# Delta stage of a two-block kernel: inverses by pivot columns, another order of emission, and low weight halves on VectorE instead of GpSimd

## The chip, the cores and the metric

The kernel runs as one program on one core of a Trainium2 chip. The metric is the device time of one execution in microseconds; less is better. The engines are TensorE (PE in the rows; PEld is its weight load), VectorE (DVE), ScalarE (ACT), GpSimd (POOL) and SyncE (SP), which here issues the DMAs. Each engine works through its own instructions in the order that was fixed when the kernel was built, and waits for other engines and DMAs by semaphores.

## The reference

Two blocks act on 512 tokens of 1024 channels, all in float32. The first has Fourier mixing with attention and a gated linear recurrence. The second has a mixer, cross attention to a memory, and a hierarchical mixture of experts. The mixer's first branch, the gated delta rule with 8 heads, is where the change lies. Cut to that:

```python
qkv = silu(causal_depthwise_conv(hn @ w_in[qkv], conv_w))
q, k = l2norm(q), l2norm(k)                 # per head, 128 wide
decay = exp(cum_i - cum_j)                  # lower triangle of a chunk of 64 tokens
a_low = where(strict, (k * beta) @ k.T * decay, 0)
sol = triangular_solve(eye + a_low, [v * beta, k * beta * exp(cum)], lower=True)
for chunk:                                  # sequential over chunks, S is 128 x 128
    v_new = u - w @ S
    o = q_dec @ S + qk_intra @ v_new
    S = S * chunk_decay + k_dec.T @ v_new
y_a = rmsnorm(o) * silu(out_gate)
```

## The kernel before

`stage_c()` (from L1019) is the mixer. Channels lie on the partitions and tokens on the free axis. A projection (`proj`, L280) is eight blocks of 128 input channels, each of three matmuls of 128 x 512, since a float32 weight and input are split into a high and a low half (`mm3`, L268): 24 matmuls into one of three PSUM banks `pj`. Other matmuls go to five banks `pm`.

**Weights.** `wget` (L255) takes the next weight block of the list `cq`, which must hold the blocks in the order in which the code asks for them; it is loaded two blocks ahead (`LC`). `wsplit` (L225) loads 128 x 1024 floats through the SyncE queue into `wr` (4 buffers), ScalarE writes the high half `wh` (L215, 4 buffers), and the difference, the low half `wl` (L217, 3 buffers), is made by VectorE, or by GpSimd for every n-th block when `wpool[0]` is n. The table `WP` sets `wpool` by sub-stage.

**The delta stage** works on two groups of four heads. `ftile(h, t)` projects head h's k (t = 1), q (0) or v (2), and runs the convolution on ScalarE and VectorE: one start `cy` on ScalarE, three multiply-adds `cy` on VectorE, a tanh, and one operation that writes `KQ` or `VF`. `p2a` makes the decay triangle `E` (GpSimd at L1132 and L1144), `p2` transposes `KQ` on TensorE (L1156), and makes the product `MI` of k with [k, q]; its 32 x 32 diagonal blocks go to DRAM (`abd`). `group_thin` works out a row of small factors for the group, `nr` among them, in some twenty operations of 16 or 32 elements a partition.

`inverse(g)` inverts the 128 unit lower triangular blocks of 32 x 32 that a group has, one in each partition: `nr` is transposed on TensorE (L1200), goes through DRAM and comes back as `rb`, the blocks come back as `AB`, and `AB` is scaled by `rb` on VectorE. Then the rows of the inverse `xr` (name `xrow`) are filled, two at a time. It is a Python generator: `over(steps, g)` emits a step of other work (a projection and what follows it), and then as many pieces of the inverse as the table `IV` (`pace`) gives for that kind of step. At the end `xt` goes to DRAM (`xd`) and comes back by eight DMAs as blocks in `X1T`.

`merges(g)` joins the 32-blocks into the inverses of 128-blocks with small matmuls. `chain(g)` is the sequential part, four chunks `c` of 128 tokens: transposes of `VF` (L1302), `vb` on VectorE, the product with `X1T` (L1314), `vn` on ScalarE, the state `St` and the output; each step needs the one before. `ofac`, `og(h)` (the output gate's projection and its `sg`) and `finish(h)` (the `y`) complete a head. `fproj(h)`, `vproj(hp)` and the projections Q are those of the next branch (HGRN); its heads follow in `hhead`. In `vproj` the weight is the moving operand: 96 matmuls of 256 columns.

**What sets the order.** The code's order of emission is not the order on an engine: a scheduler places instructions by their dependencies and an estimate of times as it builds the program, each engine's list apart. `pin()` (L265) keeps what is emitted under it behind the last projection matmul emitted. Work without dependencies on the inverse can so fill TensorE while VectorE inverts, and fill the gaps of the chain ("filler matmuls").

Of the kernel before, what the change touches and what calls it, by code (L numbers as in the profile page):

```python
# [6 lines left out]
F32 = mybir.dt.float32  # L7
# [5 lines left out]
AX = mybir.AxisListType  # L13
# [8 lines left out]
LC = [2]  # L22
IV = [2, 2, 3, 2, 1, 1]
XB = [2, 1]
# [24 lines left out]
TL = [0]  # L49
WP = [3, 1, 0, 1, 0, 0]  # L50
VP = [2]
# [113 lines left out]
def build(tc, a, stages="A", dbg=None):  # L165
# [42 lines left out]
    def mul(o, x, y):  # L208
        dve.tensor_tensor(o, x, y, op=MUL)  # L209
# [55 lines left out]
    def pin(on=True):  # L265
        return tc.issue_after(lastmm[0].ins) if on else ExitStack()
# [752 lines left out]
    def stage_c():  # L1019
# [10 lines left out]
        cq.extend([F_(4, 1), F_(4, 0), F_(4, 2), F_(5, 1), F_(5, 0), F_(5, 2), O_(0), O_(1)])  # L1030
        cq.extend([O_(2), O_(3), F_(6, 1), F_(6, 0), F_(7, 1), F_(7, 0)])
        cq.extend([P_(h) for h in range(4)] + [O_(4), O_(5), O_(6), F_(6, 2), F_(7, 2), O_(7)])
        cq.extend(V_(0) + V_(1) + [Q_(0), Q_(1)] + [Q_(2), Q_(3)] + [P_(h) for h in range(4, 8)] + V_(2))
        for i in range(4):
# [5 lines left out]
        def fproj(h):  # L1040
# [3 lines left out]
            act.activation(TH[h], ps, AF.Tanh, scale=0.5)  # L1044

        with tc.tile_pool(name="cg", bufs=1, reuse_waits="tile") as G:
            RS = ExitStack()
            R2 = RS.enter_context(tc.tile_pool(name="cr", bufs=1, reuse_waits="tile", side="right"))
            AB = R2.tile([128, 32, 32], F32, name="AB")
            vb0, ab = CAB  # L1050
# [146 lines left out]
            def inverse(g):  # L1197
# [226 lines left out]
            steps = [(fproj, 0), (fproj, 1), (fproj, 2), (fproj, 3), (og, 4), (og, 5), (og, 6), (ftile, 6, 2)]  # L1424
            for _ in range(PI[2]):
                st = steps.pop(0)
                st[0](*st[1:])
            p2(7)
# [3 lines left out]
            for _ in range(PI[3]):
                st = steps.pop(0)
                st[0](*st[1:])
            with pin(PI[3]):
# [15 lines left out]
        with tc.tile_pool(name="ch", bufs=1, reuse_waits="tile") as Hh:  # L1451
# [14 lines left out]
            v3 = lambda z: z.rearrange("p (c i) -> p c i", c=4)  # L1466
            VT, LF = {}, {}

            def vproj(hp):
                VT[hp] = R3.tile([128, 4, 256], F32, name="vt", tag="vt", bufs=2)  # L1470
                w = [wget("wci", 4 * k + hp, k) for k in range(2)]
                for tp in range(2):
                    ps = (psm if VP[0] >> hp & 1 else psj)()
                    for t in range(2):
                        tt = 2 * tp + t
                        mm3(ps[:, t * 256:t * 256 + 256],
                            [((X[k][0][:, tt * 128:tt * 128 + 128], X[k][1][:, tt * 128:tt * 128 + 128]),
                              (w[k // 4][0][:, (k % 4) * 256:(k % 4) * 256 + 256],
                               w[k // 4][1][:, (k % 4) * 256:(k % 4) * 256 + 256])) for k in range(8)])
                    act.activation(VT[hp][:, 2 * tp:2 * tp + 2, :], ps.rearrange("p (t n) -> p t n", t=2), AF.Copy)  # L1480

# [797 lines left out]
```

## Time and profile before

| | |
|---|---|
| runs | 2199.89, 2196.14, 2195.3 us; median 2196.14 |
| profiled execution | 2199.17 us; span 2197.3 us |
| TensorE busy in the span | 2104.1 us, 96% |
| VectorE busy | 1306.4 us, 59% |
| ScalarE busy | 866.3 us, 39% |
| GpSimd busy | 250.3 us, 11% |

The span is what the profiler saw from the first to the last instruction; the execution's own time is a little longer. Times in the trace count from the span's start. The change touches the stretch from about 790 to 1160 us: the first group's tiles, the first inverse (from 881), merges(0) and chain(0) (to 999), the second group's last tiles (to 1033), the second inverse (to 1092), merges(1), chain(1) (from 1113) and the start of the next branch (from 1138). In a timeline row "[3.30 <-DVE ort]" is the time the engine stood idle before it, and whose result ended that.

### The profile page before, as it was taken

The page shows a single profiled execution, that of the slowest core. Times are in us where ns is not written, and L with a number is a line of the kernel's source. Part 1 is how long each engine was busy: PE and PEld are TensorE (multiplying, and loading weights), DVE is VectorE, ACT ScalarE, POOL GpSimd, SP SyncE. Part 2 cuts the span into 40 slices and gives each one's busy share as a digit, 9 for nine tenths or more (in the row PEclk, how much of TensorE's full clock was granted, in tenths as well). Part 3 has the DMA queues.
Part 4 walks back from the last instruction along what each step waited for, and adds up shares of the span by engine and source line. Part 5 has one row for each costly group of instructions (what it writes and reads, how often), then busy time and mean ns, then how long its engine had stood idle before and what let it go on. Part 6 is the DMA issues. An engine that isn't in the chain of part 4 may idle for free. (4 is left out here: it accounts for less than half of the span.)

```text
span 2197.3 us, 28137 instructions
## 1 busy us (share of the span) xinstructions
PE 2104.1 (96%) x10806; PEld 1581.4 (72%) x10806; DVE 1306.4 (59%) x2282; ACT 866.3 (39%) x1562; POOL 250.3 (11%) x164
## 2 busy tenths in 40 slices
PE   8899999999999999898899999999999999999997
PEld 6788888788787888686788886888876544444443
DVE  7777677878858866857856454325654333333334
ACT  4444435488848664323236533223442011111002
POOL 3300000300101253423300000100001000000000
PEclk9999999999999999999999999999999999999998
DMA  5422222432322542221311225333426899999993
GB/s 178 129 63 87 68 68 72 144 101 87 115 91 64 174 129 94 70 69 47 105 54 62 80 95 167 108 100 114 133 109 265 346 411 420 420 421 421 421 420 116
DMA packets 96242, 364.65 MB, mean 166 GB/s; under 512 B 19298, under 2 KB 24804, under 8 KB 71652
## 3 DMA queue, kind: packets, MB, share of 16 engines
q1 hardware_dynamic: 94068, 359.36, 44.7%
q10 hardware_dynamic: 2032, 3.41, 0.5%
q8 instruction: 87, 1.43, 0.3%
q14 instruction: 55, 0.45, 0.1%
HBM read 348.56 MB, written 11.55 MB: 164 GB/s over the span
## 5 line engine op out<-in xcount | busy, mean ns | idle before, releaser
L271 PE MATMUL pj<-xh,wh 128*128 128x512 f32 x1136 | 448.6, 395 | 9.4 <-ACT wh L215 3.9
L273 PE MATMUL pj<-xh,wl 128*128 128x512 f32 x1136 | 447.3, 394 | 4.5 <-DVE wl L217 4.5
L272 PE MATMUL pj<-xl,wh 128*128 128x512 f32 x1136 | 445.7, 392 | 0.0
L215 ACT ACTIVATE wh<-wr 128x1024 fp32r<-128x1024 f32 (+1 forms) x269 | 263.1, 981 | 460.0 <-PE pj L272 279.8
L217 DVE TENSOR_TENSOR wl<-wr,wh 128x1024 fp32r<-128x1024 f32 (+1 forms) x242 | 277.8, 1149 | 159.6 <-PE pj L273 69.0
L271 PEld LDWEIGHTS pj<-xh,wh 128*128 128x128 f32 x1136 | 214.7, 189 | 56.3 <-ACT wh L215 5.6
L273 PEld LDWEIGHTS pj<-xh,wl 128*128 128x128 f32 x1136 | 214.6, 189 | 50.3 <-DVE wl L217 6.5
L272 PEld LDWEIGHTS pj<-xl,wh 128*128 128x128 f32 x1136 | 214.5, 189 | 43.5 <-DVE xl L217 0.7
L2046 PE MATMUL pj<-we,xe 128*64 128x512 f32 x1024 | 225.0, 594 | 0.0
L2046 PEld LDWEIGHTS pj<-we,xe 128*64 128x64 f32 x1024 | 71.4, 137 | 140.5 <-issue 137.8
L1991 DVE TENSOR_TENSOR mo<-mo,pm 128x512 f32<-128x512 f32 x128 | 80.9, 683 | 78.6 <-PE pm L1990 78.6
L2046 PE MATMUL pj<-we,hT 128*64 128x512 f32 x512 | 113.4, 595 | 0.4 <-ACT hT L1977 0.4
L2046 PEld LDWEIGHTS pj<-we,hT 128*64 128x64 f32 x512 | 35.4, 137 | 66.8 <-issue 63.9
L217 POOL TENSOR_TENSOR wl<-wr,wh 128x1024 fp32r<-128x1024 f32 x27 | 69.0, 2559 | 117.9 <-PE pj L273 86.6
L1977 ACT ACTIVATE hT<-pm 128x512 f32<-128x512 f32 x16 | 9.6, 598 | 175.7 <-PE pm L1975 175.7
L1939 PE MATMUL pm<-dk,xh 128*128 128x256 f32 x256 | 65.3, 295 | 0.0
L1939 PE MATMUL pm<-dk,xl 128*128 128x256 f32 x256 | 63.8, 289 | 0.0
L1967 ACT ACTIVATE th<-pj,ws 128x512 f32<-128x512 f32 x16 | 11.0, 689 | 126.6 <-PE pj L2046 125.5
L2039 POOL TENSOR_TENSOR we<-mo,we 128x512 f32<-128x512 f32 x4 | 5.0, 1292 | 488.0 <-DVE mo L1991 488.0
L1982 ACT ACTIVATE ye<-pj,ws 128x512 fp32r<-128x512 f32 x32 | 22.0, 689 | 95.3 <-PE pj L2046 95.3
L209 DVE TENSOR_TENSOR th<-th,pj 128x512 f32<-128x512 f32 x16 | 11.0, 688 | 80.1 <-PE pj L2046 80.1
L212 DVE SCALAR_TENSOR_TENSOR cy<-pj,vec,cy 128x509 f32<-128x509 f32 (+2 forms) x72 | 53.6, 744 | 8.5 <-ACT cy L1113 7.5
(622 smaller groups left out, 4335.7 us busy)
## 6 DMA issues: line engine op xcount, KB each, us to landing
we<-in_eg SPq DMA_DIRECT2D x64, 1024.0 KB, 10.3
we<-in_eu SPq DMA_DIRECT2D x64, 1024.0 KB, 10.1
we<-in_ed SPq DMA_DIRECT2D x63, 1024.0 KB, 12.9
wr<-in_wc SPq DMA_DIRECT2D x72, 512.0 KB, 3.6
wr<-in_wa SPq DMA_DIRECT2D x34, 512.0 KB, 3.7
wr<-in_wb SPq DMA_DIRECT2D x32, 512.0 KB, 3.7
wr<-in_wbr SPq DMA_DIRECT2D x16, 512.0 KB, 3.6
wr<-in_wao SPq DMA_DIRECT2D x8, 512.0 KB, 4.2
```

Of the source, the lines that this page charges most:

```text
L209: dve.tensor_tensor(o, x, y, op=MUL)
L212: dve.scalar_tensor_tensor(o, x, s, y, op0=op0, op1=op1)
L215: act.activation(hi, x, AF.Copy, scale=1.0 if scale is None else scale)
L217: (eng or dve).tensor_tensor(lo, x, f(hi), op=SUB)
L271: pe.matmul(ps, lh, rh, start=first and i == 0, stop=False)
L272: pe.matmul(ps, lh, rl, start=False, stop=False)
L273: lastmm[0] = pe.matmul(ps, ll, rh, start=False, stop=last and i == n - 1)
L1939: pe.matmul(ps[:, (c & 1) * 256:(c & 1) * 256 + n], HN[t, c // 4][i % 2][:, (c % 4) * 128:(c % 4) * 128 + 128], dk[t // 2][:, t % 2, :n], ...
L1967: act.activation(th, pg, AF.Tanh, scale=ws[:, 2:3])
L1982: act.activation(Y[0], py, AF.Copy, scale=ws[:, 1:2])
L1991: dve.tensor_tensor(acc[t, hf], acc[t, hf], ps, op=ADD)
L2046: last[0] = pe.matmul(ps[64 * e:64 * e + 64], lhs(k, e), wt[k // 2][:, 2 * e + k % 2, :], start=k == 0, stop=k == n - 1)
```

## The change

Three things change in the delta stage. No matmul is added or taken away.

1. `inverse` fills `xr` column by column: for each pivot j, all rows below j take the product of column j of `AB` with row j of `xr`, added in one product (L209) and one addition. That is 62 operations on (31 - j)(j//2 + 1) elements in place of sixteen products and sixteen sums on 4m x m elements (m from 1 to 16) and of the first pairing of `AB` (one product, one addition, two fills). The product's tile moves from the tag `St` to the tag `tmp`, of which there are seven buffers.
2. `WP` turns GpSimd's share of the low halves off after the first group's tiles: 17 low halves go to VectorE.
3. The order of emission: `fproj(0)` and `fproj(1)` stand inside chain(0), `fproj(2)`, `fproj(3)`, `finish(0)` and `finish(1)` among the last tiles of the second group; `ftile(7, 2)` and `vproj(0)` go into the second inverse, ahead of merges(1); `p2(6)`, `p2(7)` and the first piece of each inverse are pinned. `vproj`'s result shares two buffers with `AB`.

```diff
-IV = [2, 2, 3, 2, 1, 1]
+IV = [2, 2, 3, 2, 1, 2]
-WP = [3, 1, 0, 1, 0, 0]
+WP = [3, 0, 0, 0, 0, 0]
...
+        def vproj(hp):
+            VT[hp] = R2.tile([128, 4, 256], F32, name="vt", tag="vt", bufs=2)
...
-            AB = R2.tile([128, 32, 32], F32, name="AB")
+            AB = R2.tile([128, 32, 32], F32, name="AB", tag="vt", bufs=2)
...
                 mul(AB, AB, rb.unsqueeze(1).to_broadcast([128, 32, 32]))
-                ABf = AB.rearrange("p j i -> p (j i)")
-                dve.memset(ABf[:, 0:1024:33], 0.0)
-                pt = G.tile([128, 32, 16], F32, name="prod", tag="tmp", bufs=NT[0])
-                mul(pt, AB[:, :, 0::2], ABf[:, 1:1024:66].unsqueeze(1).to_broadcast([128, 32, 16]))
-                dve.tensor_tensor(AB[:, :, 1::2], AB[:, :, 1::2], pt, op=ADD)
-                dve.memset(ABf[:, 0:1024:33], 1.0)
...
-                prod = G.tile([128, 1024], F32, name="prod", tag="St", bufs=1)
-                for i in range(0, 32, 2):
-                    n, m = i + 2, i // 2 + 1
-                    pr = prod[:, :m * 2 * n].rearrange("p (c r j) -> p c r j", c=m, r=2)
-                    mul(pr, xr[:, :n, :m].rearrange("p j c -> p c j").unsqueeze(2).to_broadcast([128, m, 2, n]),
-                        AB[:, :n, i:i + 2].rearrange("p j r -> p r j").unsqueeze(1).to_broadcast([128, m, 2, n]))
-                    dve.reduce_sum(xr[:, i:i + 2, :m].rearrange("p r c -> p c r"), pr, axis=AX.X)
-                    yield
+                prod = G.tile([128, 512], F32, name="prod", tag="tmp", bufs=NT[0])
+                for j in range(31):
+                    n, m = 31 - j, j // 2 + 1
+                    pr = prod[:, :n * m].rearrange("p (i c) -> p i c", c=m)
+                    mul(pr, AB[:, j, j + 1:32].unsqueeze(2).to_broadcast([128, n, m]),
+                        xr[:, j:j + 1, :m].to_broadcast([128, n, m]))
+                    dve.tensor_tensor(xr[:, j + 1:, :m], xr[:, j + 1:, :m], pr, op=ADD)
+                    if j & 1:
+                        yield
+                yield
...
+            ftile(4, 0)
             inv = inverse(0)
-            if PI[0]:
-                ftile(4, 0)
-            with pin(PI[0]):
+            with pin():
                 adv(inv, 1)
...
-            over(((ftile, 4, 0),) * (1 - PI[0]) + ((ftile, 4, 2), (ftile, 5, 1), (p2, 4), (p2a, 5), (ftile, 5, 0), (ftile, 5, 2)) +
-                 (((og, 0), (p2, 5)) if PI[1] else ((p2, 5), (og, 0))) + ((og, 1), (og, 2), (og, 3)), inv)
+            over(((ftile, 4, 2), (ftile, 5, 1), (p2, 4), (p2a, 5), (ftile, 5, 0), (ftile, 5, 2), (og, 0), (og, 1),
+                  (p2, 5), (og, 2), (og, 3)), inv)
             adv(inv, 99)
             wpool[0] = WP[2]
             merges(0)
-            adv(chain(0), 99)
-            fc = ofac(0)
+            ch = chain(0)
+            adv(ch, 1)
+            fproj(0)
+            adv(ch, 1)
+            fproj(1)
+            adv(ch, 99)
             ftile(6, 1)
             p2a(6)
             ftile(6, 0)
+            fc = ofac(0)
             ftile(7, 1)
-            p2(6)
+            with pin():
+                p2(6)
             p2a(7)
             ftile(7, 0)
...
+            finish(0, fc)
+            fproj(2)
+            with pin():
+                p2(7)
             group_thin(1)
+            finish(1, fc)
+            fproj(3)
             wpool[0] = WP[3]
             inv = inverse(1)
...
-            over([(finish, h, fc) for h in range(4)] + steps, inv)
+            over(((finish, 2, fc), (finish, 3, fc), (og, 4), (og, 5), (og, 6), (ftile, 6, 2), (ftile, 7, 2), (vproj, 0)), inv)
             adv(inv, 99)
             wpool[0] = WP[4]
-            ftile(7, 2)
...
             merges(1)
             adv(chain(1), 99)
             og(7)
```

How instructions move shows best in three places. In the order's rows a number stands first, then the line, the operation, and what it writes and reads.

GpSimd, from the first group's last tiles to merges(1), before (`m1t` belongs to merges, the four `Gm` and `E` to p2a):

```order
69 L217 TENSOR_TENSOR wl<-wr,wh 128x1024 x3
70 L1132 TENSOR_TENSOR Gm<-c_78,gls_7361 128x512
71 L1132 TENSOR_TENSOR Gm<-c_78,gls_7362 128x512
72 L217 TENSOR_TENSOR wl<-wr,wh 128x1024
73 L1144 TENSOR_TENSOR E<-E,c_78 128x512
74 L217 TENSOR_TENSOR wl<-wr,wh 128x1024 x4
75 L1244 TENSOR_TENSOR m1t<-MI,c_78 128x512 x4
76 L1218 MEMSET X1T 128x2048
77 L1132 TENSOR_TENSOR Gm<-c_78,gls_7361 128x512
78 L1132 TENSOR_TENSOR Gm<-c_78,gls_7362 128x512
79 L1144 TENSOR_TENSOR E<-E,c_78 128x512
80 L217 TENSOR_TENSOR wl<-wr,wh 128x1024
```

and the same stretch after the change:

```order
65 L1147 TENSOR_TENSOR Gm<-c_78,gls_7361 128x512
66 L1147 TENSOR_TENSOR Gm<-c_78,gls_7362 128x512
67 L1159 TENSOR_TENSOR E<-E,c_78 128x512
68 L1147 TENSOR_TENSOR Gm<-c_78,gls_7361 128x512
69 L1147 TENSOR_TENSOR Gm<-c_78,gls_7362 128x512
70 L1159 TENSOR_TENSOR E<-E,c_78 128x512
71 L1255 TENSOR_TENSOR m1t<-MI,c_78 128x512 x4
72 L1227 MEMSET X1T 128x2048
73 L1147 TENSOR_TENSOR Gm<-c_78,gls_7361 128x512
74 L1147 TENSOR_TENSOR Gm<-c_78,gls_7362 128x512
75 L1159 TENSOR_TENSOR E<-E,c_78 128x512 x2
76 L1255 TENSOR_TENSOR m1t<-MI,c_78 128x512 x4
```

All the `wl` of this stretch are gone from GpSimd's list (seven more follow in row 82 of before); the others keep their order.

VectorE at the start of the first inverse (`AB` by `rb` is its first operation, `prod` and `xrow` are the recurrence), before:

```order
1046 L209 TENSOR_TENSOR AB<-AB,rb 128x1024
1047 L1212 MEMSET AB 128x32
1048 L209 TENSOR_TENSOR prod<-AB 128x512
1049 L212 SCALAR_TENSOR_TENSOR cy<-pj,vec,cy 128x509
1050 L1215 TENSOR_TENSOR AB<-AB,prod 128x512
1051 L212 SCALAR_TENSOR_TENSOR cy<-pj,vec,cy 128x510
1052 L1216 MEMSET AB 128x32
1053 L212 SCALAR_TENSOR_TENSOR cy<-pj,vec,cy 128x511
1054 L209 TENSOR_TENSOR prod<-xrow,AB 128x4
1055 L1227 TENSOR_REDUCE xrow<-prod 128x2
1056 L209 TENSOR_TENSOR prod<-xrow,AB 128x16
1057 L1227 TENSOR_REDUCE xrow<-prod 128x2x2
```

and after:

```order
1055 L209 TENSOR_TENSOR AB<-AB,rb 128x1024
1056 L212 SCALAR_TENSOR_TENSOR cy<-pj,vec,cy 128x511
1057 L209 TENSOR_TENSOR prod<-AB,xrow 128x31
1058 L1236 TENSOR_TENSOR xrow<-xrow,prod 128x31
1059 L209 TENSOR_TENSOR prod<-AB,xrow 128x30
1060 L217 TENSOR_TENSOR wl<-wr,wh 128x1024
1061 L212 SCALAR_TENSOR_TENSOR VF<-cy 128x512
1062 L1236 TENSOR_TENSOR xrow<-xrow,prod 128x30
1063 L212 SCALAR_TENSOR_TENSOR cy<-pj,vec,cy 128x509
1064 L209 TENSOR_TENSOR prod<-AB,xrow 128x58
1065 L212 SCALAR_TENSOR_TENSOR cy<-pj,vec,cy 128x510
1066 L1236 TENSOR_TENSOR xrow<-xrow,prod 128x29x2
```

The recurrence now begins right behind the scaling, in pairs of a product and an addition, and low halves (`wl`) stand between them; there are six of them up to `xt` in the first inverse, and four in the second.

TensorE in chain(1), its second chunk (`vb,X1T` and `St,KQ` are the chain's, L271 to L273 filler matmuls of a projection), before:

```order
4602 L271 MATMUL pj<-wh,xh 128x256
4603 L272 MATMUL pj<-wl,xh 128x256
4604 L273 MATMUL pj<-wh,xl 128x256
4605 L271 MATMUL pj<-wh,xh 128x256
4606 L272 MATMUL pj<-wl,xh 128x256
4607 L1314 MATMUL pm<-vb,X1T 128x128
4608 L1320 MATMUL pm<-St,KQ 128x128
4609 L1314 MATMUL pm<-vb,X1T 128x128 x3
4610 L1320 MATMUL pm<-St,KQ 128x128 x3
4611 L273 MATMUL pj<-wh,xl 128x256
4612 L1325 MATMUL pm<-vn,KD 128x128 x4
4613 L1336 MATMUL pm<-vn,MI 128x128 x4
```

and after (chain lines have moved by eleven):

```order
4665 L1336 MATMUL pm<-vn,KD 128x128 x4
4666 L1347 MATMUL pm<-vn,MI 128x128 x4
4667 L1313 MATMUL pm<-c_78,VF 128x128 x4
4668 L1319 MATMUL pm<-St,KQ 128x128 x4
4669 L1325 MATMUL pm<-vb,X1T 128x128
4670 L1331 MATMUL pm<-St,KQ 128x128
4671 L1325 MATMUL pm<-vb,X1T 128x128 x2
4672 L1331 MATMUL pm<-St,KQ 128x128
4673 L1325 MATMUL pm<-vb,X1T 128x128
4674 L1331 MATMUL pm<-St,KQ 128x128 x2
4675 L1336 MATMUL pm<-vn,KD 128x128 x4
4676 L1347 MATMUL pm<-vn,MI 128x128 x4
```

The fillers are gone from here, and from the three other chunks too: before, 47 filler matmuls stand in chain(1), after, none. In chain(0) it is the other way: seven before, all in its first chunk, and 30 after, in all four.

## Rows read from the trace of the kernel before

**Rows 1.** page, part 1: busy us (share of the span), instructions

```profile
PE 2104.1 (96%) x10806; PEld 1581.4 (72%) x10806; DVE 1306.4 (59%) x2282; ACT 866.3 (39%) x1562; POOL 250.3 (11%) x164
```

**Rows 2.** stretches: us; busy (count) of PE, PEld, DVE, ACT, POOL; clock

```profile
881.00:954.00 73.00, 65.09 (x280) 52.98 (x279) 61.27 (x82) 23.64 (x58) 33.32 (x15) 0.95 0.26 77
975.40:999.60 24.20, 21.21 (x163) 18.79 (x161) 14.24 (x40) 9.63 (x38) 2.04 (x2) 1.00 0.07 23
999.60:1033.30 33.70, 24.85 (x111) 19.97 (x112) 28.37 (x60) 14.91 (x54) 12.33 (x7) 0.95 0.15 44
1033.30:1092.10 58.80, 52.37 (x250) 44.58 (x249) 48.91 (x57) 14.78 (x20) 20.39 (x9) 0.94 0.35 108
1112.90:1137.70 24.80, 24.80 (x202) 23.66 (x201) 14.65 (x38) 10.87 (x39) 0.55 (x2) 1.00 0.14 43
```

**Rows 3.** PE's waits, 880 to 1150 us: total us, times, longest

```profile
PE pm L1156 <- DVE KQ L212: 7.5, 4, 3.0
PE pj L271 <- DVE cy L212: 6.4, 1, 6.4
PE pm L1200 <- DVE ort L209: 3.3, 1, 3.3
PE pj L271 <- DVE oss L1357: 2.7, 1, 2.7
PE pm L1200 <- DVE nr L212: 2.3, 1, 2.3
```

**Rows 4.** shorter stretches, columns as in rows 2

```profile
885.00:888.50 3.50, 3.50 (x10) 2.73 (x9) 0.11 (x1) 0.00 (x0) 0.00 (x0) 0.51 0.47 107
1011.40:1014.80 3.40, 2.91 (x9) 2.58 (x10) 2.27 (x5) 1.15 (x8) 0.00 (x0) 0.50 0.47 159
1083.00:1089.90 6.90, 5.18 (x24) 5.21 (x25) 5.49 (x7) 2.58 (x4) 2.66 (x2) 0.51 0.55 143
1050.00:1060.00 10.00, 10.00 (x46) 8.26 (x45) 9.50 (x15) 3.73 (x5) 5.21 (x2) 1.00 0.40 131
```

**Rows 5.** timeline of POOL and DVE: start us, us, engine, line, operation

```profile
880.86 2.38 POOL L217 TENSOR_TENSOR wl<-wr,wh 128x1024 fp32r<-128x1024 f32 x1 [1.45 <-DVE rstg L212]
881.06 2.22 DVE L209 TENSOR_TENSOR rstg<-rsyg 128x32 f32<-128x32 f32 x1
1008.30 0.69 DVE L209 TENSOR_TENSOR VF<-VF,ort 128x512 f32<-128x512 f32 x1
1008.91 2.84 DVE L212 SCALAR_TENSOR_TENSOR KQ<-cy 128x512 f32<-128x512 f32 x1
```

**Rows 6.** POOL's groups, 880 to 1150 us: busy us, mean ns; idle, releaser

```profile
L217 POOL TENSOR_TENSOR wl<-wr,wh 128x1024 fp32r<-128x1024 f32 x16 | 42.0, 2625 | 61.8 <-PE pj L273 47.3 <-issue 7.5 <-DVE ort L209 3.8
L1144 POOL TENSOR_TENSOR E<-E,c 128x512 f32<-128x512 f32 x3 | 4.8, 1584 | 8.1 <-ACT E L1143 8.1
```

**Rows 7.** DVE's groups, 1040 to 1079 us (second inverse)

```profile
L209 DVE TENSOR_TENSOR prod<-xrow,AB 128x4 f32<-128x4 f32 (+15 forms) x16 | 19.7, 1233 | 0.5
L1227 DVE TENSOR_REDUCE xrow<-prod 128x2 f32<-128x4 f32 (+15 forms) x16 | 8.7, 544 | 0.5
L209 DVE TENSOR_TENSOR AB<-AB,rb 128x1024 f32<-128x1024 f32 x1 | 3.5, 3467 | 6.9 <-DMA AB<-abd 6.9
```

**Rows 8.** DVE timeline, second inverse: its second pair, its last product

```profile
1049.60 0.19 DVE L209 TENSOR_TENSOR prod<-xrow,AB 128x16 f32<-128x16 f32 x1
1049.82 0.17 DVE L1227 TENSOR_REDUCE xrow<-prod 128x4 f32<-128x16 f32 x1
1074.93 2.12 DVE L209 TENSOR_TENSOR prod<-xrow,AB 128x1024 f32<-128x1024 f32 x1
```

**Rows 9.** DVE's low halves, 1150 to 1200 us

```profile
L217 DVE TENSOR_TENSOR wl<-wr,wh 128x1024 fp32r<-128x1024 f32 x6 | 7.3, 1220 | 3.7 <-PE pm L272 3.7
```

**Rows 10.** from the second inverse's end to its stacked blocks (DVE, SP queue)

```profile
1078.34 0.59 DVE L1230 COPY xt<-xrow 128x512 f32<-128x512 f32 x1
1081.07 5.17 SPq L1234 DMA_DIRECT2D X1T<-xd  x8
```

More of the change, by code (lines that the diff above doesn't have):

```diff
@@ L1030, in stage_c @@
         cq.extend([F_(4, 1), F_(4, 0), F_(4, 2), F_(5, 1), F_(5, 0), F_(5, 2), O_(0), O_(1)])
-        cq.extend([O_(2), O_(3), F_(6, 1), F_(6, 0), F_(7, 1), F_(7, 0)])
-        cq.extend([P_(h) for h in range(4)] + [O_(4), O_(5), O_(6), F_(6, 2), F_(7, 2), O_(7)])
-        cq.extend(V_(0) + V_(1) + [Q_(0), Q_(1)] + [Q_(2), Q_(3)] + [P_(h) for h in range(4, 8)] + V_(2))
+        cq.extend([O_(2), O_(3), P_(0), P_(1), F_(6, 1), F_(6, 0), F_(7, 1), F_(7, 0), P_(2), P_(3)])
+        cq.extend([O_(4), O_(5), O_(6), F_(6, 2), F_(7, 2)] + V_(0) + [O_(7)])
+        cq.extend(V_(1) + [Q_(0), Q_(1)] + [Q_(2), Q_(3)] + [P_(h) for h in range(4, 8)] + V_(2))
         for i in range(4):
@@ L1044, in fproj @@
             act.activation(TH[h], ps, AF.Tanh, scale=0.5)
+        RS = ExitStack()
+        R2 = RS.enter_context(tc.tile_pool(name="cr", bufs=1, reuse_waits="tile", side="right"))
+        VT = {}
+        def vproj(hp):
+            VT[hp] = R2.tile([128, 4, 256], F32, name="vt", tag="vt", bufs=2)
+            w = [wget("wci", 4 * k + hp, k) for k in range(2)]
+            for tp in range(2):
+                ps = (psm if VP[0] >> hp & 1 else psj)()
+                for t in range(2):
+                    tt = 2 * tp + t
+                    mm3(ps[:, t * 256:t * 256 + 256],
+                        [((X[k][0][:, tt * 128:tt * 128 + 128], X[k][1][:, tt * 128:tt * 128 + 128]),
+                          (w[k // 4][0][:, (k % 4) * 256:(k % 4) * 256 + 256],
+                           w[k // 4][1][:, (k % 4) * 256:(k % 4) * 256 + 256])) for k in range(8)])
+                act.activation(VT[hp][:, 2 * tp:2 * tp + 2, :], ps.rearrange("p (t n) -> p t n", t=2), AF.Copy)
         with tc.tile_pool(name="cg", bufs=1, reuse_waits="tile") as G:
-            RS = ExitStack()
-            R2 = RS.enter_context(tc.tile_pool(name="cr", bufs=1, reuse_waits="tile", side="right"))
-            AB = R2.tile([128, 32, 32], F32, name="AB")
+            AB = R2.tile([128, 32, 32], F32, name="AB", tag="vt", bufs=2)
             vb0, ab = CAB
@@ L1396, in stage_c @@
             wpool[0] = WP[1]
+            ftile(4, 0)
             inv = inverse(0)
-            if PI[0]:
-                ftile(4, 0)
-            with pin(PI[0]):
+            with pin():
                 adv(inv, 1)
-            pace = {ftile: IV[0], og: IV[1], fproj: IV[2], p2: IV[3], p2a: 0, finish: IV[4]}
+            pace = {ftile: IV[0], og: IV[1], fproj: IV[2], p2: IV[3], p2a: 0, finish: IV[4], vproj: IV[5]}
             def over(steps, g):
@@ L1419, in stage_c @@
             ftile(6, 0)
+            fc = ofac(0)
             ftile(7, 1)
-            p2(6)
+            with pin():
+                p2(6)
             p2a(7)
             ftile(7, 0)
[L1424 to L1428, printed above, removed]
+            finish(0, fc)
+            fproj(2)
+            with pin():
+                p2(7)
             group_thin(1)
+            finish(1, fc)
+            fproj(3)
             wpool[0] = WP[3]
             inv = inverse(1)
[L1432 to L1435, printed above, removed]
+            with pin():
                 adv(inv, 1)
-            over([(finish, h, fc) for h in range(4)] + steps, inv)
+            over(((finish, 2, fc), (finish, 3, fc), (og, 4), (og, 5), (og, 6), (ftile, 6, 2), (ftile, 7, 2), (vproj, 0)), inv)
             adv(inv, 99)
             wpool[0] = WP[4]
-            ftile(7, 2)
-            RS.close()
-            R3 = RS.enter_context(tc.tile_pool(name="cv", bufs=1, reuse_waits="tile", side="right"))
             merges(1)
@@ L1466, in stage_c @@
             v3 = lambda z: z.rearrange("p (c i) -> p c i", c=4)
[L1467 to L1480, printed above, removed]
+            LF = {}
             def logs(g):
@@ L1566, in hfinish @@
                 nc.sync.dma_start(ybd[h], y)
-            vproj(0)
             vproj(1)
```

## The prediction

> **What bounds the kernel now.** I read the page's busy shares first: TensorE is busy for 96% of the span [rows 1], so time can be won only where it stands still or runs at half clock. Then I cut the delta stage into its pieces and asked for busy time by stretch [rows 2]: length less TensorE's busy time is 7.9 us in the first inverse (881 to 954), 3.0 in chain(0), 8.9 in the second group's tiles (999.6 to 1033.3), 6.4 in the second inverse and none in chain(1). The waits [rows 3] name what ends each: always VectorE, though TensorE waits for it by different names. `KQ` is waited for four times, `nr` and `ort` once each ahead of the transpose of `nr`, `oss` and `cy` because VectorE has not yet released a projection bank. Behind long waits the granted clock falls to its lower level, 1.2 GHz [rows 4]: there are two such stretches in the first inverse (the one shown and one alike behind the `KQ` wait at 919 us), one at 1011, one at 1083. Half of the busy time in them is lost: 1.7 and 1.7, 1.45 and 2.6 us.
>
> So TensorE loses 7.9 + 3.4 = 11.3 us around the first inverse, 3.0 in chain(0), 8.9 + 1.45 = 10.3 in the second tiles, 6.4 + 2.6 = 9.0 before merges(1). What VectorE does in these places is the question.
>
> **Low halves move off GpSimd.** In 880 to 1150 us GpSimd makes 16 low halves at 2.6 us [rows 6]; a seventeenth is ahead of it. Beside them VectorE operations on SBUF operands last as long as the GpSimd one still runs: a 32-element operation takes 2.22 us beside a low half of 2.38, and a `KQ` of 512 elements 2.84 where the operation of the same size just before took 0.69 [rows 5]. Three of the waits follow from such a pair. The sixteen products of the second inverse show the same: 19.7 us [rows 7], of which I work out 14.0 below. Moved, a low half costs VectorE 1.22 us [rows 9], 17 of them 21 us. GpSimd keeps `Gm`, `E` and `m1t`; an `E` of 1.6 us [rows 6] can still block VectorE once.
>
> **The inverse.** The prices come from two groups [rows 5, 8]. A product of 16 elements takes 0.19 us and the next operation starts 0.22 after it, so about 0.16 is fixed and 0.03 a gap. The product of 1024 takes 2.12: 1.91 ns an element, with operands that step through rows. The 512-element product with one operand repeated along the inner axis takes 0.69 [rows 5]: 1.04 ns an element. Before, per group: sixteen products of 5984 elements in all, 11.4 + 16 x 0.19 = 14.5 us; sixteen sums 8.7 + 0.5 of gaps [rows 7]; and the pair product 1.14, its addition 0.69 and two fills, 0.3 with gaps: 25.8 us. After: 31 pivots of a product and an addition, 62 x 0.19 = 11.8 us, and twice 2856 elements (the sum of (31-j)(j//2+1)) at 1.04 ns, 5.9: 17.7 us. If the new products ran at the old ones' 1.91 ns it would be 20.2. I take 17.7, since their operands are contiguous or repeated as in the 0.69 us row; the additions' strided ones at j = 0 and 1 have 61 elements.
>
> The Trainium skill says in "SBUF — State Buffer" (section "Specifications (TRN2)") that SBUF is accessed in lines of 16 bytes and that each step into a new line pays. The old products step 64 or 128 bytes an element and the new ones do not, so by that rule the sum is the 17.7, and by the old products' row the 20.2; the two slopes above agree with it.
>
> Against the change speaks that 34 operations of the recurrence become 62: 28 more x 0.19 = 5.3 us, in the 17.7 already. The Trainium skill, "VectorE: DVE Perf Modes" (section "Rules for kernel authors"), says to keep the number of operations down, since the pipe is flushed after each. By the count alone the inverse would grow; the rows show the fixed share of an operation to be 0.19.
>
> **Does X1T now come in time?** From the order: in the first inverse VectorE does, from the scaling of `AB` to `xt`, 1.2 + 17.7 + 10 `cy` at 0.66 of pitch + 6 low halves at 1.14 + 13 other operations of 0.5 to 0.7, together about 41 us. `AB` can start some 7 us after the transpose of `nr` (it waited 6.9 us for its DMA [rows 7]). From `xt` to the last of the eight block transfers are 7.9 us (1078.34 to 1086.24 [rows 10]), and I allow 2 for landing: 58 us. TensorE's cover after that transpose is 254 projection matmuls at 0.217 (46 in 10 us [rows 4]), 55 us, and two p2 of some 2.5: 60. In the second inverse VectorE has about 33 us (17.7, 1.2, four low halves, six `cy`, seven others), so `X1T` comes 50 us after the transpose; the cover is 180 projection matmuls, 96 of half width and two heads' transposes, 39 + 10.4 + 2 = 51 to 53. Both just fit, with about 2 us to spare. Before, the cover of the second gave out because `cy` stood behind the inverse in VectorE's order.
>
> **The sum, by stretch.** First inverse: 11.3 goes; 1.6 stays for an `E` beside the thin operations and 0.7 for a low half that TensorE meets half done: -9.0. Chain(0): 30 fillers cover its 3.0: -3.0. Chain(1): it loses all its fillers. Chain(0) with seven of them took 24.2 us for 21.2 busy [rows 2], so an empty one stands 3.0 + 7 x 0.217 = 4.5: +4.5. Second tiles: 10.3 goes; the 2.3 of `nr` stays, since some fifteen small dependent operations stand ahead of the transpose as before, and one low half of 1.2: -6.8. Second inverse: 9.0 goes; the low halves of the next two projections stand behind `xt`, 1.2 each: -6.6. What comes after chain(1): the HGRN heads have 26 filler matmuls less, 5.6 us of cover; nothing if it covered no wait, 5.6 if all, plus a low half of 1.2 behind the chain. I take 2 + 1.2, below the middle, since some of the filler only sits there: +3.2. The SyncE queue keeps its order but for one weight load between `xd` and the blocks, which I count at nothing, since its buffer is free a projection earlier; were it not, a low half's 1.2 us is its price. The shared `vt` buffers cost nothing, as vproj(0) takes the second one. Together -17.7 us.
>
> The profiled execution took 2199.17, so 2181.5 in its terms; the runs' median is 2196.14, which gives **2178.4**. Ends: nothing left over and no loss in the heads, -29.1, 2167; all leftovers doubled, the heads at their 6.8 and products at 20.2, -5, 2191. I count a gain here in full at the end, since TensorE is busy for nearly the whole span.
>
> **Rivals.** *VectorE is full.* The two slacks are 2 us. If its operations there come to 8 us more in each group (blocked by `E` and `Gm`, or waiting for ScalarE's copies), TensorE stands 6 us before each merge, and comes back at half clock for another 1.7 and 2.6: 16.3 back, 2195. For it: VectorE was busy 61 of 73 and 49 of 59 us already, and gets low halves on top. Against: 8 us per inverse and the blocked time go.
>
> *Low halves hold up VectorE (slower).* A low half must wait until TensorE has done with one of three `wl` buffers. On GpSimd 47.3 us of idle before 16 of them ended that way, 3.0 each [rows 6], and hurt nobody; on VectorE the inverse stands behind. At the 3.0 of that row six and four of them make `X1T` late by 18 - 2 and 12 - 2 us, and half clock adds 4.3: +30.3 against -17.7, 2209. It decides for slower from 2.2 us a low half on (10 x 2.2 - 4 + 4.3 = 22.3, more than 17.7 + 4.4). Against: where VectorE makes them now it waited 3.7 us before six [rows 9], 0.6 each, and the order places them among the pivots.
>
> *The change does not do what it says.* The transposes of `nr` and the `KQ` ones stand at the same distance behind VectorE's work as before; if that order and not GpSimd makes those waits, the first and third term fall away and -1.9 is left: 2194.
>
> *More operations cost more than fewer elements save (slower too).* If an element's price didn't fall, the inverse would take 25.8 + 5.3 = 31 us, `X1T` come 13 - 2 us late twice, and half clock add 4.3: 26 back, 2205. The rule on the number of operations (the Trainium skill, as above) points this way; the slopes [rows 5, 8] speak against it.
>
> **Chances.** Forecast 0.67, full VectorE 0.11, held-up VectorE 0.11, no effect 0.09, dear operations 0.02. A measurement of this kernel tells about 0.2%, 4.4 us, from no change. Faster takes the forecast and a part of the first rival: 0.71; same 0.16; slower 0.13. Reaching to 2197 leaves out the slow rivals and the tails: 2167 to 2197. The forecast's own range is 2167 to 2191.
>
> **What would show it.** Right: 62 operations of 0.19 to 0.4 us in each inverse, 18 us in sum; no VectorE operation of over 1.5 us in either; no `KQ` wait of 3 us; TensorE's wait at the first L271 ahead of merges(1) under 2 us and no half clock there; 4 to 5 us of waits in chain(1). Wrong: VectorE waiting for TensorE at `wl` inside an inverse; TensorE idle ahead of the merges for `X1T`; products near 1.9 ns an element; waits of over 7 us in the heads after chain(1), which would take from the gain what the inverses give.

## The result and the profile after

The changed kernel takes 2174.39 us (median of four runs, 2173.2 to 2176.76); the kernel before takes 2196.07 on the same chip. The ratio is 0.9897, 95% interval 0.9881 to 0.9913: 21.7 us or 1.0% faster, 4.0 us below the forecast. The two profiled executions, 2199.17 and 2173.2, are 26.0 us apart. Of these 23.3 are in the changed stretch, as worked out below; 1.7 are in a wait before the expert stage (4.2 us before, 2.5 after, at a line that the change does not touch; two further executions with the change's code there show 2.8 and 1.4, and what sets it stays open). The first profiled execution was one of the slower runs of its kernel, so sizes below are those of stretches, not of spans.

The page, part 1, of the changed kernel:

```profile
PE 2097.5 (97%) x10806; PEld 1575.9 (73%) x10806; DVE 1285.5 (59%) x2351; ACT 866.6 (40%) x1562; POOL 204.9 (9%) x147
```

Busy time by stretch, columns as in [rows 2]; the stretches are the first inverse, chain(0), the second tiles, the second inverse, chain(1) and the 24 us behind it:

```profile
881.00:946.40 65.40, 64.13 (x293) 53.06 (x292) 52.53 (x118) 24.89 (x60) 10.44 (x7) 1.00 0.36 107
967.80:992.00 24.20, 24.20 (x184) 22.17 (x183) 13.25 (x37) 9.55 (x37) 1.47 (x1) 1.00 0.13 44
992.00:1021.10 29.10, 27.82 (x135) 22.34 (x133) 28.22 (x66) 14.84 (x54) 6.08 (x5) 1.00 0.28 86
1021.10:1077.40 56.30, 54.27 (x287) 46.06 (x287) 40.24 (x90) 17.18 (x23) 7.76 (x4) 1.00 0.40 123
1098.40:1122.20 23.80, 19.07 (x152) 17.34 (x151) 12.59 (x37) 8.51 (x37) 0.56 (x2) 1.00 0.07 23
1122.20:1146.20 24.00, 21.23 (x144) 18.66 (x144) 16.08 (x43) 12.76 (x28) 0.00 (x0) 1.00 0.30 98
```

Length less TensorE's busy time: 1.3, 0, 1.3, 2.0, 4.7 and 2.8 us. The granted clock is 1.00 in each, and it is 1.00 throughout from 870 to 1160 us: none of the four half-clock stretches that the prediction counts, three of them in [rows 4], is left. What TensorE waited for, 880 to 1150 us:

```profile
PE pm L1325 <- DVE vb L212: 2.5, 3, 1.3
PE pm L1384 <- DVE VF L209: 1.9, 2, 1.5
PE pj L273 <- DVE wl L217: 1.4, 1, 1.4
PE pm L1171 <- DVE KQ L212: 1.3, 2, 0.9
PE pm L1215 <- DVE nr L212: 1.3, 1, 1.3
```

Beside [rows 3]: `KQ` from 7.5 to 1.3 us, `nr` and `ort` together from 5.6 to 1.3, `oss` and `cy` gone. New are chain(1)'s `vb`, one low half, and `VF` in `finish`, right behind chain(1).

### The profile page after: what moved, and what is told of

Read it like the earlier page. It is cut to its first block, busy times and chain, and to the rows that moved or that the text cites. A ratio compares the mean times of both kernels' runs of the same rounds, so it can differ in the third digit from the quotient of the medians.

```text
span 2171.4 us, 28195 instructions
## 1 busy us (share of the span) xinstructions
PE 2097.5 (97%) x10806; PEld 1575.9 (73%) x10806; DVE 1285.5 (59%) x2351; ACT 866.6 (40%) x1562; POOL 204.9 (9%) x147
## 5 line engine op out<-in xcount | busy, mean ns | idle before, releaser
L271 PE MATMUL pj<-xh,wh 128*128 128x512 f32 x1136 | 448.1, 394 | 5.9 <-ACT wh L215 3.4
L273 PE MATMUL pj<-xh,wl 128*128 128x512 f32 x1136 | 446.7, 393 | 6.1 <-DVE wl L217 5.9
L217 DVE TENSOR_TENSOR wl<-wr,wh 128x1024 fp32r<-128x1024 f32 (+1 forms) x259 | 298.1, 1152 | 169.6 <-PE pj L273 77.2
L271 PEld LDWEIGHTS pj<-xh,wh 128*128 128x128 f32 x1136 | 214.1, 188 | 52.3 <-ACT wh L215 5.1
L273 PEld LDWEIGHTS pj<-xh,wl 128*128 128x128 f32 x1136 | 214.0, 188 | 52.4 <-DVE wl L217 8.4
L209 DVE TENSOR_TENSOR th<-th,pj 128x512 f32<-128x512 f32 x16 | 11.0, 689 | 80.1 <-PE pj L2043 80.1
L1936 PEld LDWEIGHTS pm<-dk,xh 128*128 128x128 f32 x256 | 50.3, 197 | 5.7 <-issue 5.7
L1986 PE MATMUL pm<-ye,DT 128*128 128x512 f32 x128 | 54.1, 424 | 0.0
## 6 DMA issues: line engine op xcount, KB each, us to landing
we<-in_eg SPq DMA_DIRECT2D x64, 1024.0 KB, 10.6
we<-in_eu SPq DMA_DIRECT2D x64, 1024.0 KB, 10.6
```

The source lines that it names most:

```text
L217: (eng or dve).tensor_tensor(lo, x, f(hi), op=SUB)
L271: pe.matmul(ps, lh, rh, start=first and i == 0, stop=False)
L273: lastmm[0] = pe.matmul(ps, ll, rh, start=False, stop=last and i == n - 1)
L1936: pe.matmul(ps[:, (c & 1) * 256:(c & 1) * 256 + n], HN[t, c // 4][i % 2][:, (c % 4) * 128:(c % 4) * 128 + 128], dk[t // 2][:, t % 2, :n], ...
L1986: pe.matmul(ps, DT[:, t * 128:t * 128 + 128], Y[0], start=True, stop=False)
```

## The experiments

**Which part brings it.** Each combination of the three parts was run, each beside the kernel before on the same chip. "Pivot" is the new inverse, "lows" the low halves on VectorE, "order" the new emission with its pins and list.

| kernel | us (median) | ratio to before, interval | against before |
|---|---|---|---|
| lows | 2191.15 | 0.9970, 0.9957 to 0.9982 | -5.1 |
| pivot | 2193.04 | 0.9982, 0.9973 to 0.9992 | -3.2 |
| order | 2192.13 | 0.9986, 0.9973 to 0.9998 | -4.7 |
| order, pivot | 2186.09 | 0.9953, 0.9937 to 0.9969 | -10.7 |
| order, lows | 2186.69 | 0.9960, 0.9938 to 0.9981 | -10.1 |
| pivot, lows | 2174.73 | 0.9895, 0.9877 to 0.9912 | -22.1 |
| all three (again) | 2173.66 | 0.9895, 0.9880 to 0.9910 | -22.8 |

The edits are those of the change, taken alone or left out: lows is the line of `WP`, pivot the body of `inverse`, order everything else.

Lows alone:

```diff
-WP = [3, 1, 0, 1, 0, 0]
+WP = [3, 0, 0, 0, 0, 0]
```

> The kernel before with nothing changed but the low halves, 17 of which go to VectorE. Theory A: blocked time of some 8 to 11 us an inverse goes, 20.7 us of low halves come, so VectorE gains little in the inverses; the waits at nr and KQ (together some 7 us with half clock) go, the stall ahead of merges(1) stays or grows by 1 to 4 us: 2 to 7 us faster, 2189 to 2194. Theory B: no difference or slower, 2195 to 2205.

5.1 us faster, within theory A's 2 to 7. The waits behind GpSimd's low halves are gone, and others stand in their place:

```profile
PE pj L271 <- DVE xrow L1227: 4.7, 1, 4.7
PE pj L271 <- DVE cy L212: 4.3, 1, 4.3
PE pm L1200 <- DVE nr L212: 1.3, 1, 1.3
```

Both long ones are projection banks that VectorE, busy with low halves and the old inverse, releases late, one at each inverse. The one of 4.3 us is the stall ahead of merges(1): it was 6.4 and has shrunk, where theory A had it stay or grow. The one of 4.7 us, at 900, is new; the profile puts it down to `xrow`, but the operation that reads the bank is the `cy` just before that.

Pivot alone:

```diff
-                for i in range(0, 32, 2):
...
+                for j in range(31):
...
+                    dve.tensor_tensor(xr[:, j + 1:, :m], xr[:, j + 1:, :m], pr, op=ADD)
```

> The kernel before with nothing changed but the inverse (pivot form). Theory A: 6 to 8 us a group off VectorE; the cy that the stall ahead of merges(1) waits for stands behind the inverse and comes that much sooner, so the 6.4 + 2.6 us there go to 0 to 2, nr and KQ waits stay: 6 to 10 us faster, 2186 to 2190. Theory B: more blocking of 62 short operations by GpSimd eats it: under 3 us, 2193 to 2197.

3.2 us faster by the median, in theory B's band and not the 6 to 10 us of A; the profiled execution, 2187.7 us, was the quickest of ten and lies in A's band, so its trace shows the better case, and what made the others some 5 us longer stays open. Its waits are the mirror of the last ones:

```profile
PE pm L1156 <- DVE KQ L212: 3.9, 2, 3.0
PE pm L1200 <- DVE ort L209: 3.3, 1, 3.3
PE pm L1200 <- DVE nr L212: 2.4, 1, 2.4
PE pm L1243 <- DMA X1T<-xd: 1.5, 1, 1.5
PE pm L1248 <- ACT X L1244: 2.3, 3, 2.0
```

The stall of 6.4 us ahead of merges(1) has shrunk to waits of 1.5 (`X1T`) and 2.0 (`X`), and those behind GpSimd's low halves stay.

Order alone, and order with one of the others:

> The new order alone: old inverse, low halves shared with GpSimd as before. Theory A: chain(0) gains 3 and chain(1) loses 4.7; the blocked time and the long inverse together overrun the slack by 10 us or more in each group: no gain or a loss against the kernel before, 2190 to 2200. Theory B: nearly the whole gain is there, 2174 to 2180. If the parts simply add (C), the sum of this, of low halves alone and of the pivot inverse alone gives the 21.7 us.

> The change without its low halves: every second or third part of them back on GpSimd as before (WP as before), pivot inverse and new order kept. Theory A (each part acts through VectorE's time: a low half of 2.6 us on GpSimd holds VectorE's SBUF operations up; the shorter inverse takes 8 us a group off VectorE; the order covers chain(0) and takes cy out from behind the inverse): X1T slack is 4.6 and 4.2 us in the trace after; about 8 us of blocking per inverse overruns it by some 3.5 us each, with half clock behind, and KQ or nr waits of 2 to 3 us come back: 8 to 12 us above the changed kernel, 2182 to 2186. Theory B (the order brings nearly all, GpSimd's low halves hurt little): within 3 us of the changed kernel, 2174 to 2177.

> The change without the pivot inverse: old row-pair inverse in the new order, low halves on VectorE. Theory A: the inverse is 6 to 8 us longer, X1T's slack is 4.6 and 4.2 us, so TensorE waits 2 to 3.5 us ahead of each merge and runs at half clock behind: 6 to 11 us above the changed kernel, 2180 to 2185. Theory B: the cover is enough or the order makes room elsewhere: under 3 us, 2174 to 2177.

Order alone gives 4.7 us: inside A's band of 2190 to 2200, though A said no gain. The two kernels that have the order and one of the other parts lie 11.7 and 12.3 us above the change (A said 8 to 12 and 6 to 11), so B, that the order brings nearly all, is out. With order alone 10.6 us of waits for banks that `cy` holds remain, 7.9 of them in one ahead of merges(1). C is out too: 5.1 + 3.2 + 4.7 = 13.0 is not 21.7.

Pivot and lows in the old order:

> The kernel before in its old order, with the pivot inverse and the low halves on VectorE. Theory A: the waits for nr and KQ beside GpSimd's low halves go (some 7 us), the stall of 6.4 us and half clock of 2.6 ahead of merges(1) shrinks since the cy behind the inverse comes 8 us or more sooner; chain(0) stays: 10 to 16 us faster than before, 2180 to 2186. Theory B: under 5 us faster, above 2191.

22.1 us faster, more than theory A said, and as fast as the whole change. So the new order adds nothing that can be measured once the other two are there. In this kernel's trace TensorE waits 3.9 us in chain(0), and here:

```profile
PE pj L271 <- DVE oss L1353: 2.7, 1, 2.7
PE pm L1200 <- DVE nr L212: 1.3, 1, 1.3
PE pj L273 <- DVE wl L217: 0.9, 1, 0.9
```

Of these the new order takes away `oss` and the 3.4 us at the lower clock level behind it (994.7 to 998.2, granted 0.51); `nr` is 1.3 in the change too, and a low half is waited for there as well. But here chain(1) has its fillers and one wait of 0.9, for a low half of theirs, where the change has 4.7 us; and the second inverse has none, where the change has 2.0.

**Is filler a fixed stock?** Of the new order only chain(0)'s filling, on top of pivot and lows:

```diff
-            adv(chain(0), 99)
+            ch = chain(0)
+            adv(ch, 1)
+            fproj(0)
+            adv(ch, 1)
+            fproj(1)
+            adv(ch, 99)
```

> The kernel with pivot inverse and low halves in the old order, and of the new order only fproj(0) and fproj(1) inside chain(0) (and ofac(0) two steps later). Theory A (a fixed stock of filler: chain(0) gains its 3.9 us and the 2.7 us wait and 1.7 of half clock behind it, the second inverse and chain(1) lose the filler): chain(1) 4 to 5 us of waits again, in all 2171 to 2175, within 2 us of that kernel. Theory B (chain(0) was lost time for want of order alone): 6 to 8 us faster than it, 2166 to 2169.

2178.84 us (ratio 0.9920, 0.9907 to 0.9934): 4 us slower than without it (the two intervals just touch), where A expected no difference and B a gain. Chain(0) is covered, but a wait stands ahead of merges(1), with half clock behind it (1061.7 to 1068.5, granted 0.50), and chain(1) is bare again:

```profile
PE pj L271 <- DVE cy L212: 3.3, 1, 3.3
```

From 870 to 1200 us its waits and what half clock costs come to 17.4 us, against 13.2 for pivot and lows alone, which is the 4 us of the medians. The reading is that two projections taken from the second inverse were missed there.

Filler for chain(1), first by copying og(7) out of its bank:

```diff
-OE = [4, 5, 6]
+OE = [4, 5, 6, 7]
```

> The changed kernel with og(7) also in OE: its projection is copied out of its bank by ScalarE at once, so that chain(1) has a bank for 22 filler matmuls (none in the change). Theory A (chain(1)'s 4.7 us of waits are for want of filler, and filler is not missed later): 2 to 4 us faster than the changed kernel, 2170 to 2172. Theory B (the heads behind chain(1) miss the 22 matmuls, which are moved, not added): the waits come back there, within 1.5 us of the changed kernel.

2174.10 us (0.9899, 0.9882 to 0.9915): no difference, theory B, but not in B's place. Chain(1) keeps one wait of 1.7 us; behind it, TensorE has run out of what it can do and waits for `finish`:

```profile
PE pm L1384 <- DVE VF L209: 5.5, 1, 5.5
PE pm L1325 <- DVE vb L212: 1.7, 1, 1.7
```

Then by projecting vproj(1) into the banks `pj`:

```diff
-VP = [2]
+VP = [0]
```

> The changed kernel with vproj(1) in the projection banks, not in the five others (VP 2 to 0). It is then placed ahead of merges(1), its banks are free again at once, and filler matmuls stand in all chunks of chain(1). Theory A (chain(1)'s 4.7 us of waits come from banks that og(7) and two projections of the next branch hold): 3 to 4.5 us faster than the changed kernel, 2170 to 2171. Theory B (filler is a fixed stock: what stands in chain(1) is missing in the heads behind): waits there grow by 2 to 4 us, within 1.5 us of the changed kernel.

2177.68 us (0.9915, 0.9901 to 0.9928): 4.0 slower than the change on the same chip, whose interval it overlaps by a little, where A expected a gain and B no difference. Chain(1) has no wait left, and this stands behind it:

```profile
PE pj L271 <- DVE qc L212: 9.7, 1, 9.7
```

VectorE's timeline shows what TensorE waits behind: all filler has been used up before the next branch's heads can start, and their first scan waits for a load.

```profile
1140.26 1.23 DVE L1497 TENSOR_TENSOR_SCAN cum<-cmk,LF 128x512 f32<-128x512 f32 x1 [4.04 <-DMA cmk<-in_cmask]
```

Behind the wait 17 us run at the lower level (1135.2 to 1152.2, granted 0.50, 8.1 busy, so some 4 lost). The load of `cmk` is issued at 1135.8 us, when TensorE is waiting already, and at 1133.6 in the change; it takes 4.3 us to land. What the missing filler costs and what the load costs is therefore not told apart; an earlier load was not tried.

**What holds VectorE up.** Sixteen GpSimd subtractions that nobody needs, in the second inverse of the change:

```diff
+                    if g == 1 and j < 16:
+                        pool.tensor_tensor(gz, ABf[:, 0:480], ABf[:, 512:992], op=SUB)
```

> The changed kernel with sixteen extra GpSimd subtractions of 480 elements (both inputs in SBUF) in the second inverse, into a tile that nothing reads; nothing waits for them but GpSimd's own next work, which has over 10 us to spare. The output is the same. Theory A (GpSimd and VectorE hold each other up when both read SBUF twice): VectorE loses up to 1 us beside each, 8 to 14 us in all, X1T's slack of 4.2 us is overrun: 4 to 12 us slower than the changed kernel with half clock behind the wait. Theory B (it was only that GpSimd's low halves came late for TensorE, not the blocking): no difference, under 1.5 us.

2191.85 us (0.9982, 0.9973 to 0.9992): 17.5 slower than the change, beyond theory A's upper end. GpSimd's timeline, then VectorE's:

```profile
1030.79 22.48 POOL L1235 TENSOR_TENSOR gz<-AB 128x480 f32<-128x480 f32 x16 [20.52 <-DVE AB L209]
...
1034.86 1.23 DVE L1240 TENSOR_TENSOR xrow<-xrow,prod 128x30 f32<-128x30 f32 x1
1036.12 1.26 DVE L209 TENSOR_TENSOR prod<-AB,xrow 128x58 f32<-128x58 f32 x1
1037.42 1.27 DVE L1240 TENSOR_TENSOR xrow<-xrow,prod 128x58 f32<-128x58 f32 x1
...
1076.72 0.61 DVE L1245 COPY xt<-xrow 128x512 f32<-128x512 f32 x1
```

The recurrence's short operations take nearly as long as a GpSimd operation (1.4), whatever their own length, as if the two took turns; a low half between them kept its 1.2 us. `xt` comes 15.1 us later than in the change. But TensorE waits nowhere for `X1T`, the place that A's sum had. In the same inverse low halves stand behind the recurrence in VectorE's order, and TensorE waits for these, twice in the inverse (5.5 and 2.8 us) and once more ahead of merges(1) (3.5):

```profile
PE pj L272 <- DVE wl L217: 8.3, 2, 5.5
PE pj L273 <- DVE wl L217: 4.9, 2, 3.5
```

That is 11.8 us more than the 1.4 of the change; three stretches at the lower level with 12.3 us of busy time cost another 6.1, together 17.9 for the 17.5 measured.

The same inverse with GpSimd busy as long, but only filling the tile (behind one subtraction of 8 elements, which ties the fills to `AB`):

```diff
+                    if g == 1 and j < 16:
+                        if j == 0:
+                            pool.tensor_tensor(gz[:, 0:8], ABf[:, 0:8], ABf[:, 512:520], op=SUB)
+                        for _ in range(3):
+                            pool.memset(gz, float(j))
```

> As the run with sixteen extra GpSimd subtractions in the second inverse, but with 48 GpSimd fills of the same tile (480 elements, no input read) behind one subtraction of 8 elements, so that GpSimd is busy for some 20 us of that inverse without reading SBUF. The output is the same. Theory A (what holds VectorE up is GpSimd's reading through a way both share): short VectorE operations stay at 0.2 to 0.3 us and the time within 1.5 us of the changed kernel. Theory B (any GpSimd work on SBUF holds VectorE up): VectorE operations of 0.4 us and more beside the fills, 3 to 12 us slower.

2173.41 us (0.9897, 0.9882 to 0.9912), no difference from the change. GpSimd and VectorE:

```profile
1030.53 26.74 POOL L1238 MEMSET gz<- 128x480 f32 x48
...
1034.14 0.22 DVE L1243 TENSOR_TENSOR xrow<-xrow,prod 128x58 f32<-128x58 f32 x1
1034.40 0.22 DVE L209 TENSOR_TENSOR prod<-AB,xrow 128x56 f32<-128x56 f32 x1
```

So theory A holds in its narrow form: what holds VectorE up is a GpSimd operation that reads SBUF, not GpSimd at work. The Trainium skill, "SBUF — State Buffer" (section "SBUF: two separate sides"), says this of a pair of ports that the two engines take for a whole instruction, for VectorE operations with two SBUF inputs against GpSimd operations that read SBUF; the 1.2 us beside subtractions and the 0.22 beside fills agree.

The change itself, as the measure on the chip of three of these runs (chain(0)'s filling, vproj(1) in `pj`, the fills):

> The changed kernel itself, as the measure for the three others on this chip: 2172 to 2177.

2173.66 us.

## Why the prediction was right, step by step

**The sum by stretch** was 17.7 us, and the rows give 23.3 for the same terms.

| term | forecast | by the rows |
|---|---|---|
| first inverse | -9.0 | 11.3 to 1.3: -10.0 |
| chain(0) | -3.0 | 3.0 to 0: -3.0 |
| chain(1) | +4.5 | 0 to 4.7: +4.7 |
| second tiles | -6.8 | 10.3 to 1.3: -9.0 |
| second inverse | -6.6 | 9.0 to 2.0: -7.0 |
| behind chain(1) | +3.2 | 1.8 to 2.8: +1.0 |

Two terms were mis-sized. In the second tiles I let the 2.3 us of `nr` stay, "since some fifteen small dependent operations stand ahead of the transpose as before". They do, and 17 filler matmuls cover them, 15 before; `nr` itself was held beside GpSimd's low half. Before, then after:

```profile
1030.51 2.34 POOL L217 TENSOR_TENSOR wl<-wr,wh 128x1024 fp32r<-128x1024 f32 x1 [6.35 <-issue]
1030.58 2.30 DVE L212 SCALAR_TENSOR_TENSOR nr<-a,rsyg 128x16 f32<-128x16 f32 x1
...
1020.84 0.17 DVE L212 SCALAR_TENSOR_TENSOR nr<-a,rsyg 128x16 f32<-128x16 f32 x1
```

In all four kernels with the low halves on VectorE (lows alone, with either part, and the change) the second transpose does not wait at all, in all four with GpSimd's share (before, pivot, order, order and pivot) it waits 2.3 to 2.4 us. Behind chain(1) I charged 26 missing filler matmuls at 2.0 us and a low half at 1.2; of the waits found there, 1.9 are for `VF` and 0.7 for `qc`, and 1.8 were there before, of this stretch:

```profile
1137.70:1161.70 24.00, 22.24 (x150) 19.40 (x148) 14.36 (x40) 11.67 (x25) 0.00 (x0) 1.00 0.26 82
```

Between the two medians the gain is 21.7, so some 1.6 of the stretch's 23.3 is the profiled executions' difference or is given back later; which, the runs do not tell.

**The inverse's price** was 17.7 us. Where nothing blocks it, as with pivot and lows in the old order, its 62 operations take this:

```profile
L1221 DVE TENSOR_TENSOR xrow<-xrow,prod 128x126 f32<-128x126 f32 (+22 forms) x31 | 7.9, 255 | 0.9
L209 DVE TENSOR_TENSOR prod<-AB,xrow 128x126 f32<-128x126 f32 (+22 forms) x31 | 7.9, 254 | 0.9
```

7.9 + 7.9 and 1.8 of gaps, 17.6 us. So 1.04 ns an element and 0.19 fixed were right, the strided price of 20.2 was not met, and the rival of dear operations falls. In the change it is 9.0 + 8.9 + 1.6 = 19.5 in the second inverse: two operations of 1.3 and 1.4 us stand beside `m1t` on GpSimd. In the first it is 19.2, with four operations of over 0.4 us (0.42, 0.70, 0.80 and 1.33). So in both inverses a few operations lie outside my mark of 0.19 to 0.4, and the sum is over the 18 that I marked. My mark "no VectorE operation of over 1.5 us" fails in the first inverse alone, at `xt`, 1.7 us beside an `m1t`.

**Does X1T come in time?** I had 2 us to spare in each group. In the second:

```profile
1061.57 0.62 DVE L1241 COPY xt<-xrow 128x512 f32<-128x512 f32 x1
...
1064.94 5.99 SPq L1245 DMA_DIRECT2D X1T<-xd  x8
...
1077.38 1.03 PE L1258 MATMUL pm<-c,X1T 128*128 128x128 f32 x8
```

The last block's transfer is issued by 1070.9 and TensorE takes it at 1077.4; with 2.3 us to landing that is 4.2 to spare, and 4.5 in the first group. The forecast had `X1T` 58 and 50 us after the transpose; it was 59 and 52, and the cover 63 and 56 instead of 60 and 53. I had expected that the two kernels 12 us above the change overrun this. Their traces do not show it. `xt` comes there at 1075.9 us (order and lows) and 1076.0 (order and pivot), some 14 us later than in the change, and yet TensorE waits for `X1T` only once, 0.9 us; its longer waits are for other results of VectorE. In order and pivot, then in order and lows:

```profile
PE pj L271 <- DVE xrow L1236: 3.8, 1, 3.8
PE pm L1258 <- DMA X1T<-xd: 0.9, 1, 0.9
...
PE pj L273 <- DVE wl L217: 6.4, 2, 5.0
```

The scheduler also places each kernel anew: in order and lows 314 matmuls stand on TensorE from the first transpose of `nr` to merges(0), in the change 290. The combinations tell what a part brings as built, not at one fixed order.

**Held-up VectorE** did not happen: between the scaling of `AB` and `xt` no low half waits for its buffer, and ahead of it one for 0.4 us. Those of 3.4 to 5.4 us that GpSimd used to have [rows 6] stand behind `xt`, where little follows:

```profile
888.30 1.23 DVE L217 TENSOR_TENSOR wl<-wr,wh 128x1024 fp32r<-128x1024 f32 x1 [0.38 <-PE pj L273]
...
937.58 1.23 DVE L217 TENSOR_TENSOR wl<-wr,wh 128x1024 fp32r<-128x1024 f32 x1 [3.40 <-PE pj L273]
943.08 1.23 DVE L217 TENSOR_TENSOR wl<-wr,wh 128x1024 fp32r<-128x1024 f32 x1 [4.27 <-PE pj L273]
```

In the second inverse one low half ahead of the scaling stands behind 4.25 us of idle that the profile puts down to no engine; the scaling waits for `rb`'s load behind it for another 1.2 us.

**What the forecast did not say** is which part carries the gain. It credited the terms to places, and chain(0) to the order. The experiments show that the order as a whole is worth nothing on top of the other two (2174.7 against 2174.4 and 2173.7): its gain in chain(0) and at `oss`, 3.9 + 2.7 us and half clock, is paid in chain(1), in the second inverse (2.0) and behind. Without the other two it is worth 5, and with one of them 5 to 7.5. That lows and pivot alone give 5.1 and 3.2 and together 22.1 is shown. The traces from 870 to 1200 us say more (columns as in [rows 2]; before, lows, pivot, both):

```profile
870.00:1200.00 330.00, 301.23 (x1812) 258.21 (x1811) 235.62 (x414) 119.59 (x330) 76.71 (x42) 0.97 0.22 69
870.00:1200.00 330.00, 308.03 (x1845) 264.71 (x1844) 234.12 (x441) 123.86 (x335) 30.56 (x25) 0.97 0.23 71
870.00:1200.00 330.00, 310.70 (x1859) 267.59 (x1858) 230.91 (x480) 129.36 (x343) 70.40 (x42) 0.97 0.23 72
870.00:1200.00 330.00, 318.50 (x1949) 275.42 (x1948) 222.80 (x500) 141.43 (x358) 29.71 (x25) 0.99 0.25 76
```

Length less TensorE's busy time is 28.8, 22.0, 19.3 and 11.5 us. So the waits nearly add: 6.8 and 9.5 less with one part, 17.3 less with both. What half clock costs, half of the busy time in the stretches at the lower level, is 7.4, 7.5, 8.0 and 1.7: no part alone takes any of it away, both together take 5.7. The rest of the surplus is pivot's: its trace shows 8.9 us won, its median 3.2. Why half clock goes only with both, and what makes pivot's other runs longer than the profiled one, stays open.

## What to carry to other kernels

Test parts of a change in combination before one is dropped or praised: two parts that brought 5 and 3 us alone brought 22 together. Look then at waits and at the clock apart; here the waits nearly added, and half clock went only with both parts. Filler work that was put into one gap was taken from another: the three tries here brought no gain and twice a loss of some 4 us, which no count of fillers told. Work shared with GpSimd can cost VectorE more than it takes off, when both read SBUF: with the pivot inverse, 17 low halves taken back from GpSimd cost VectorE 1.2 us each, and the kernel became 18 us faster (2193.0 to 2174.7).

## What was not expected of the hardware

Sixteen GpSimd subtractions of 480 elements took 22.5 us beside VectorE, 1.4 each, and the recurrence's short VectorE operations between them 1.2 to 1.3 in place of 0.2 to 0.3; the 48 fills took 26.7 us and left VectorE's at 0.22. Which waits are followed by half clock is not told by their length: `oss` at 999 us of the kernel before was waited for 2.7 us and none followed; with pivot and lows the same wait of 2.7 us was followed by 3.4 us of it; with lows alone a wait of 0.8 us at 977 us was followed by this stretch at the lower level (columns as in [rows 2]):

```profile
977.60:984.50 6.90, 6.18 (x27) 5.89 (x28) 0.00 (x0) 1.48 (x4) 0.00 (x0) 0.51 0.00 0
```

The runs do not settle what decides it.
